# Wider buffers for split weights: 4128 bytes for 4096 in a two-layer decoder kernel

## The chip, the cores and the metric

The kernel runs on 1 core of a Trainium2 chip. The metric is the device time of one execution in microseconds, as the median of the runs. TensorE (PE) multiplies matrices, VectorE (DVE) and ScalarE (ACT) work elementwise, GpSimd (POOL) does a few small things, SyncE (SP) issues the DMAs that bring the weights. All operands of TensorE lie in the on-chip memory SBUF, which has 128 partitions; a place in it is a byte offset within each partition.

## What is computed

A decoder trunk of two layers on 512 tokens of 1024 features, all float32. Each layer is a half step of SwiGLU, a mixer (a pooling branch and an attention branch with 16 heads, merged by gates), and another half step of SwiGLU:

```python
def swiglu(x, w_gate, w_up, w_down):
    return (jax.nn.silu(x @ w_gate) * (x @ w_up)) @ w_down

for l in range(DEPTH):
    x = x + 0.5 * swiglu(rmsnorm(x, ffn1_norm[l]), ffn1_w_gate[l], ffn1_w_up[l], ffn1_w_down[l])
    proj = rmsnorm(x, mix_norm[l]) @ w_in[l]      # queries, keys, values, gates, pool input
    ...
    merged = g_pool * (o_pool @ w_branch_pool[l]) + g_attn * (o_nsa @ w_branch_nsa[l])
    x = x + merged @ w_out[l]
    x = x + 0.5 * swiglu(rmsnorm(x, ffn2_norm[l]), ffn2_w_gate[l], ffn2_w_up[l], ffn2_w_down[l])
return rmsnorm(x, final_norm)
```

The hidden width of SwiGLU is 2816.

## The kernel before

Activations are kept transposed, 128 features on the partitions and the 512 tokens along the free axis. A float32 product is made of three float32r passes over two-part splits of both operands: high times high, high times low, low times high. `mm3` (lines 110 to 117) issues them for each tile of 128 input features: line 114 multiplies the high weights `wh` with the high activations, line 115 `wh` with the low activations, line 116 the low weights `wl` with the high activations. The weights are the stationary operand (128 by 128, loaded into the array by a weight load ahead of each matmul) and the activations are the moving operand (512 columns that stream through). The weight load of the next matmul runs while the present one streams.

Weights come in blocks of 1 MB: `load` (line 88) issues one DMA on SP into one of three raw buffers `wr`; `wsplit` (line 95) cuts off a unit of 8 tiles of 128 by 128 (the last chunk of SwiGLU has units of 6 for the down projection), copies its high part on ACT (line 107) into one buffer of the tag `w` and takes the low part on DVE (line 108) into another. The tag `w` has six buffers, so three units are held at a time. `proj` (line 119) makes one output tile of 128 features from a unit, 24 matmuls for a unit of 8.

The order of the work is the order in which `run_steps` goes through a list of steps written out by hand; each unit's load and split are traced ahead of the matmuls of the unit before it. Three kinds of activations stand as the moving operand against units of the tag `w`: `xh`/`xl` (the gained and split input, tag `xg`, 16 buffers of 2048 bytes; also `oh`/`ol`, the attention output), `act` (SwiGLU's hidden tiles), `mh`/`ml` and `mixed` (these three in the large buffers of tag `A`). Gate and up projections, and the mixer's input projection `w_in`, move `xh`/`xl`; the down projection moves `act`.

The allocator puts the buffers one behind another, tag by tag in the order of first use, so what stands ahead of a tag fixes its place. All tags between `s` and `x` follow one another without gaps. From the built programs, places in bytes modulo 256 (a buffer's tiles of 512 or 2048 bytes have the same place as its start, modulo 256):

| tag | what | before | with the change |
|---|---|---|---|
| `A` | `act`, `mh`/`ml`, `mixed`, probabilities | 128 | 128 |
| `ident` | matrix for transposes | 128 | 128 |
| `wr` | raw weights | 32 | 32 |
| `w` buffers 0, 1, 2, 3, 4, 5 | split weights | 32 each | 32, 64, 96, 128, 160, 192 |
| `xg` | `xh`/`xl`, `oh`/`ol` | 32 | 224 |
| `x` | residual, queries `q` | 32 | 224 |
| `K`, `pr`, `V`, `pc`, `Kc` | keys, probabilities, values | 160 | 96 |

A unit's high and low part lie in buffers 0 and 5, 4 and 3, or 2 and 1, in turn.

Of the kernel before, what the change touches and what calls it, by code (L numbers as in the profile page):

```python
# [12 lines left out]
F32R = mybir.dt.float32r  # L13
# [38 lines left out]
class Trunk:  # L52
    """Activations are kept transposed: features on partitions, the 512 tokens
    along the free axis. A float32 product is three float32r passes over exact
    two-part splits of both operands (hi*hi + hi*lo + lo*hi)."""

# [10 lines left out]

# [1 line left out]
    def unit(self, tag, bufs, dt=F32, name=None, shape=(P, T)):  # L69
# [16 lines left out]

# [1 line left out]
    def load(self, src, kt, cols):  # L88
        """Rows (k p) of a [kt*128, cols] block onto partitions p."""
        raw = self.unit("wr", 3, F32, "wr", (P, 2048))  # L90
        v = raw[:, : kt * cols].rearrange("p (k c) -> p k c", k=kt)
        self.nc.sync.dma_start(v, src.rearrange("(k p) c -> p k c", p=P))
        return v

    def wsplit(self, v):
        """Exact split of a [128, a, b] weight block, a * b <= 1024."""
        a, b = v.shape[1], v.shape[2]
        out = []
        for nm in ("wh", "wl"):
            t = self.unit("w", 6, F32R, nm, (P, 1024))  # L100
            out.append(t[:, : a * b].rearrange("p (a b) -> p a b", a=a))
        hi, lo = out
        self.split(hi, lo, v)
        return hi, lo
# [5 lines left out]
    def mm3(self, out, terms, first=True, last=True):  # L110
        """out = sum over terms of lhsT^T rhs, each given as (lh, ll, rh, rl)."""
        n = len(terms)
        for i, (lh, ll, rh, rl) in enumerate(terms):
            self.nc.tensor.matmul(out, lh, rh, start=first and i == 0, stop=False)  # L114
            self.nc.tensor.matmul(out, lh, rl, start=False, stop=False)  # L115
            self.nc.tensor.matmul(out, ll, rh, start=False,  # L116
                                  stop=last and i == n - 1)

    def proj(self, tag, w, act):
        """One 128-feature output tile from a split weight unit."""  # L120
        out = self.bank(tag)
        hi, lo = w
        self.mm3(
            out,
            [(hi[:, k], lo[:, k], act[k][0], act[k][1]) for k in range(hi.shape[1])],
        )
        return out

# [1 line left out]
    def constants(self):  # L130
# [14 lines left out]
    def load_columns(self, names):  # L145
        """Per-feature vectors as columns, 128 features on partitions."""
        nc, io = self.nc, self.io
        rows = self.s("rows")[:, :P]
        r0 = min(ROWS[nm] for nm in names)
        n = 0  # L150
        for nm in names:
            src = io[nm]
            if nm == "cmp_pos":
                src = src.rearrange("l (a b) c -> (l a) (b c)", b=2)
            elif nm == "final_norm":
                src = src.rearrange("(k c) -> k c", c=P)
            else:
                src = src.rearrange("l (k c) -> (l k) c", c=P)
            r = ROWS[nm] - r0
            n = max(n, r + src.shape[0])  # L160
            nc.scalar.dma_start(rows[r : r + src.shape[0]], src)
        pt = self.bank("pv")
        nc.tensor.transpose(pt[:, :n], rows[:n], self.ident[:n, :n])
        nc.vector.tensor_copy(self.cols[:, r0 : r0 + n], pt[:, :n])

    def constants2(self):
        nc = self.nc

        def const(shape, name):
            return self.sb.tile(list(shape), F32, tag=name, name=name)  # L170

        # dist[p, c] = 384 + p - c, and MASKED where that is negative
        self.dist = const((P, T), "dist")
# [4 lines left out]
                                channel_multiplier=1)  # L178
        # distc[(j n), t] = t - (16 n + 31), and MASKED where that is negative
        self.distc = const((P, T), "distc")  # L180
        for j in range(4):
# [5 lines left out]
                                    channel_multiplier=-16)  # L187
        # qcol[(e d), m]: negated query scale over the slope of head 2 m + e
        self.qcol = const((P, ND), "qcol")
        for h in range(H):  # L190
            e = h % 2
            nc.gpsimd.memset(self.qcol[e * DH : e * DH + DH, h // 2 : h // 2 + 1],
                             -(DH ** -0.5) / SLOPES[h])
        # block[p, j] = 1 where p // 32 is j or j + 2
        self.block = const((P, 2), "block")
        nc.gpsimd.memset(self.block, 0.0)
        for j in range(4):
            nc.gpsimd.memset(self.block[32 * j : 32 * j + 32, j % 2 : j % 2 + 1], 1.0)
        # ramp[g, t] = w / (t + 1) for the first w tokens of pool group g
        self.ramp = const((P, 4, 16), "ramp")  # L200
# [4 lines left out]

# [1 line left out]
    def gain(self, x, col):  # L207
        """Split of x times its feature gain."""
        g = self.cols[:, col : col + 1]
# [8 lines left out]
    def norm_piece(self, d, x, row, split=True):  # L218
        """x[d] is final: gain it, split it, add its squares."""
        nc = self.nc  # L220
# [14 lines left out]
    def stats(self):  # L235
        """Per token 1/rms of the last normed activation, as columns per token
        block and (but after the last layer) along rows."""
        nc = self.nc
# [36 lines left out]

# [1 line left out]
    def run_steps(self, steps, nxt=0):  # L277
        """Steps are (fetch, run); each fetch is traced ahead of the run of the
        fetching step before it."""
        fetches = [i for i, (f, _) in enumerate(steps) if f]  # L280
        for i, (_, run) in enumerate(steps):
            while nxt < len(fetches) and (nxt == 0 or fetches[nxt - 1] <= i):
                steps[fetches[nxt]][0]()
                nxt += 1
            run()

    def units(self, src, n, kt, cols, cut, use, rows=False, pre=None):
        """Steps over n weight blocks [kt*128, cols], each cut into units of
        `cut` columns (or row tiles)."""
        steps = []  # L290
# [17 lines left out]

# [1 line left out]
    def ffn(self, wg, wu, wd, on_x):  # L310
# [41 lines left out]

# [1 line left out]
    def key_cmp_in(self, j, w):  # L354
        """Compressed-branch input as [(parity d), g, token pair]."""
        p = self.proj("mm", w, self.xg)
# [8 lines left out]
    def keys(self, br, w):  # L365
        """Keys stacked twice on partitions, hi and lo apart."""
        nc = self.nc
# [12 lines left out]
    def values(self, tb):  # L380
        """Values (stationary [keys, hi | lo]) and branch gates of a token block."""
        nc = self.nc
# [48 lines left out]
    def compress_steps(self, l, which):  # L431
        """MLP over the overlapping blocks of the compressed keys (which = 0) or
        values (1), the blocks stationary as [hi | lo]."""
        nc, io = self.nc, self.io
# [82 lines left out]

# [1 line left out]
    def pool_weights(self, l):  # L519
# [7 lines left out]
    def pool_unit(self, l, g, w):  # L527
        """Pool group g: trailing mean less the token, mixed and scaled."""
        nc = self.nc
# [28 lines left out]

# [1 line left out]
    def query_unit(self, m, w):  # L560
        """Per head of the pair the negated scaled query over the head's slope,
        [hi; lo] on partitions (odd heads [lo; hi])."""
        nc = self.nc
# [10 lines left out]
    def cmp_probs(self, qd):  # L574
        """Gated probabilities over the compressed keys of four heads, per head
        pair hi and lo stacked on partitions, [hi; lo] and [lo; hi]."""
        nc = self.nc
# [39 lines left out]
    def head_probs(self, h):  # L617
        """Gated probabilities of the selected and window branches, queries on
        partitions. The selection takes every block (8 of at most 16) and the
        window spans the sequence, so both attend to all keys up to the query."""  # L620
        nc = self.nc
# [72 lines left out]

# [1 line left out]
    def mixer(self, l, on_x):  # L696
# [110 lines left out]

# [1 line left out]
    def run(self):  # L809
# [103 lines left out]
```

## Time and profile before

| | |
|---|---|
| median of 2 runs | 2411.93 us (2410.0 to 2413.85) |
| span of the profiled execution | 2409.0 us |
| TensorE, matmuls | busy 2377.3 us (99%), 11042 matmuls |
| TensorE, weight loads | busy 1951.9 us (81%) |
| VectorE | 1398.9 us (58%) |
| ScalarE | 976.9 us (41%) |
| DMA | 31.6% of 16 engines, 101 GB/s from and to HBM |
| granted TensorE clock | 0.998 of full speed |

A matmul's busy time overlaps the next one's, since matmuls are pipelined: a single one is shown 389 ns long while the next starts 227 ns after it. The time that a matmul costs in a run of them is therefore read from start to start, called the step below, and not from its length. Lengths and steps go up and down together.

### The profile page before, as it was taken

The numbers are of one execution on the slowest core, as the hardware profiler recorded it, in microseconds if no ns is written. First come the engines' busy times: TensorE is split into PE (matmuls) and PEld (weight loads), VectorE is DVE, ScalarE is ACT, GpSimd is POOL, SyncE is SP. The second block draws the span as 40 slices with busy tenths as digits, with TensorE's granted clock in tenths as the row PEclk, the third lists the DMA queues.
The fourth block names the chain that finished last, engine by engine and source line by source line (L and its number), as shares of the span: only waits on it lengthen the run. The fifth ranks groups of instructions, "written<-read, shape, count | busy, mean of one in ns | idle before, by whom it ended". The sixth has DMA issues, their size and how long they took to land.

```text
span 2409.0 us, 28552 instructions
## 1 busy us (share of the span) xinstructions
PE 2377.3 (99%) x11042; PEld 1951.9 (81%) x11042; DVE 1398.9 (58%) x2684; ACT 976.9 (41%) x1689; POOL 51.5 (2%) x106
## 2 busy tenths in 40 slices
PE   8999999999999999999999999999999999999998
PEld 6888888788888888888888888887888887888887
DVE  4434347778988544443544443567988975434444
ACT  4222234566666422222432222445666753222222
POOL 1000000000001000000000000000000010000000
PEclk9999999999999999999999999999999999999999
DMA  5332324422125422323232323335222253232321
GB/s 158 98 95 95 97 89 147 141 98 71 49 79 167 135 88 91 102 90 98 92 104 89 96 97 96 119 108 160 69 68 79 75 184 105 89 103 88 105 79 62
DMA packets 226007, 244.24 MB, mean 101 GB/s; under 512 B 8688, under 2 KB 206416, under 8 KB 225872
## 3 DMA queue, kind: packets, MB, share of 16 engines
q1 hardware_dynamic: 225696, 242.37, 31.6%
q8 instruction: 87, 1.43, 0.3%
q14 instruction: 48, 0.39, 0.1%
q10 hardware_dynamic: 176, 0.05, 0.0%
HBM read 223.53 MB, written 18.87 MB: 101 GB/s over the span
## 4 chain that ended last, share of the span: by engine, by line
PE 58%; issue 15%; DVE 1%; POOL 1%; DMA 1%; ACT 0%; POOLq 0%; DVEq 0%; SPq 0%; ACTq 0%
PE ps_mm L116 9%; PE ps_mm L115 9%; PE ps_mm L114 9%; PE ps_pv L689 4%; PE ps_sc L114 3%; PE ps_sc L115 3%; PE ps_sc L116 3%; PE ps_pt L114 3%; PE ps_pt L115 3%; PE ps_pt L116 3%; PE ps_pt L675 3%; PE ps_sc L653 2%; PE ps_sc L643 1%; DMA bP<-dB 1%; PE ps_sc L582 0%
## 5 line engine op out<-in xcount | busy, mean ns | idle before, releaser
L107 ACT ACTIVATE wh<-wr 128x1024 fp32r<-128x1024 f32 (+1 forms) x392 | 408.8, 1043 | 1099.5 <-PE ps_mm L115 414.3
L108 DVE TENSOR_TENSOR wl<-wr,wh 128x1024 fp32r<-128x1024 f32 (+1 forms) x392 | 469.9, 1200 | 76.6 <-ACT wh L107 75.5
L116 PE MATMUL ps_mm<-act,wl 128*128 128x512 f32 x704 | 280.8, 399 | 0.0
L114 PE MATMUL ps_sc<-xh,wh 128*128 128x512 f32 x704 | 277.1, 394 | 2.2 <-ACT x L838 2.2
L115 PE MATMUL ps_mm<-act,wh 128*128 128x512 f32 x704 | 277.6, 394 | 0.0
L114 PE MATMUL ps_mm<-act,wh 128*128 128x512 f32 x704 | 275.5, 392 | 0.0
L115 PE MATMUL ps_sc<-xl,wh 128*128 128x512 f32 x704 | 274.5, 390 | 0.0
L116 PE MATMUL ps_sc<-xh,wl 128*128 128x512 f32 x704 | 274.2, 389 | 0.0
L114 PE MATMUL ps_pt<-xh,wh 128*128 128x512 f32 x704 | 273.9, 389 | 0.0
L115 PE MATMUL ps_pt<-xl,wh 128*128 128x512 f32 x704 | 273.9, 389 | 0.0
L116 PE MATMUL ps_pt<-xh,wl 128*128 128x512 f32 x704 | 273.9, 389 | 0.0
L340 DVE SCALAR_TENSOR_TENSOR x<-ps_mm,x 128x512 f32<-128x512 f32 x96 | 66.4, 691 | 253.8 <-PE ps_mm L116 253.8
L331 DVE TENSOR_TENSOR u<-ps_pt,R 128x512 f32<-128x512 f32 x88 | 60.9, 692 | 245.7 <-PE ps_pt L116 245.7
L114 PE MATMUL ps_mm<-xh,wh 128*128 128x512 f32 x512 | 203.4, 397 | 0.0
L323 DVE TENSOR_TENSOR z<-ps_sc,R 128x512 f32<-128x512 f32 x88 | 60.9, 692 | 243.1 <-PE ps_sc L116 243.0
L116 PE MATMUL ps_mm<-xh,wl 128*128 128x512 f32 x512 | 200.9, 392 | 0.0
L115 PE MATMUL ps_mm<-xl,wh 128*128 128x512 f32 x512 | 200.8, 392 | 0.0
L115 PEld LDWEIGHTS ps_mm<-act,wh 128*128 128x128 f32 x704 | 132.1, 188 | 34.7 <-DVE act L108 0.8
L114 PEld LDWEIGHTS ps_sc<-xh,wh 128*128 128x128 f32 x704 | 132.4, 188 | 31.5 <-ACT x L838 2.6
L114 PEld LDWEIGHTS ps_mm<-act,wh 128*128 128x128 f32 x704 | 132.2, 188 | 31.6
L116 PEld LDWEIGHTS ps_mm<-act,wl 128*128 128x128 f32 x704 | 132.2, 188 | 30.5
L634 ACT ACTIVATE tbuf<-tbuf,m 128x128 f32<-128x128 f32 (+3 forms) x256 | 142.1, 556 | 36.3 <-DVE m L632 28.4
(238 smaller groups left out, 3864.6 us busy)
## 6 DMA issues: line engine op xcount, KB each, us to landing
wr<-in_ffn_w_gate_dram SPq DMA_DIRECT2D x44, 1024.0 KB, 5.4
wr<-in_ffn_w_up_dram SPq DMA_DIRECT2D x44, 1024.0 KB, 5.4
wr<-in_w_in_dram SPq DMA_DIRECT2D x34, 1024.0 KB, 5.3
wr<-in_ffn_w_down_dram SPq DMA_DIRECT2D x32, 1024.0 KB, 4.9
wr<-in_ffn_w_down_dram SPq DMA_DIRECT2D x16, 768.0 KB, 4.2
wr<-in_w_branch_nsa_dram SPq DMA_DIRECT2D x8, 1024.0 KB, 5.2
wr<-in_w_out_dram SPq DMA_DIRECT2D x8, 1024.0 KB, 5.3
dx<-x SPq DMA_DIRECT2D x16, 256.0 KB, 2.7
```

The costliest lines, as they stand in the source:

```text
L107: self.nc.scalar.activation(hi, src, AF.Copy)
L108: self.nc.vector.tensor_sub(lo, src, f32(hi))
L114: self.nc.tensor.matmul(out, lh, rh, start=first and i == 0, stop=False)
L115: self.nc.tensor.matmul(out, lh, rl, start=False, stop=False)
L116: self.nc.tensor.matmul(out, ll, rh, start=False, stop=last and i == n - 1)
L323: nc.vector.tensor_mul(z, g, self.R)
L331: nc.vector.tensor_mul(u, up, self.R)
L340: nc.vector.scalar_tensor_tensor(x, o, 0.5, x, ALU.mult, ALU.add)
L634: nc.scalar.activation(t, t, AF.Exp, scale=-1.0, bias=m[:, i : i + 1], accum_out=c[:, i : i + 1])
L653: nc.tensor.matmul(sp, qq, K[:, br, :nk], start=i == 0, stop=i == 1)
L675: nc.tensor.transpose(tp[:, w : w + P], probs[qb, br][:, kb * P : kb * P + P], self.ident)
L689: nc.tensor.matmul(out[:, T - n :], lhsT, rhs, start=i == 0, stop=i == len(ops) - 1)
```

## The change

Each buffer of the tag `w` gets 1032 float32 elements on a partition for 1024. The units still use the first 1024 of them (or fewer), so each instruction reads and writes as much as before. The six buffers take 192 bytes more on each partition, and all that is allocated behind them moves up by 192 bytes. Comments and docstrings are left out, and a blank line is added ahead of the changed one, so that lines from 100 on have numbers that are higher by one.

```diff
     def wsplit(self, v):
-        """Exact split of a [128, a, b] weight block, a * b <= 1024."""
+
         a, b = v.shape[1], v.shape[2]
         out = []
         for nm in ("wh", "wl"):
-            t = self.unit("w", 6, F32R, nm, (P, 1024))
+
+            t = self.unit("w", 6, F32R, nm, (P, 1032))
             out.append(t[:, : a * b].rearrange("p (a b) -> p a b", a=a))
```

On every engine the same instructions stand in the same order with the same waits, and each tile is in the buffer with the same number as before.

## Rows read from the trace of the kernel before

**Rows 1.** The page: span, and busy time of each engine

```profile
span 2409.0 us, 28552 instructions
...
PE 2377.3 (99%) x11042; PEld 1951.9 (81%) x11042; DVE 1398.9 (58%) x2684; ACT 976.9 (41%) x1689; POOL 51.5 (2%) x106
```

**Rows 2.** Stretches: gate and up; down; mixer. Columns as in the heading row

```profile
core 0: us, PE busy (x) PEld busy (x) DVE busy (x) ACT busy (x) POOL busy (x), PEclk, DMA share, GB/s
30.00:108.00 78.00, 78.00 (x347) 64.55 (x346) 35.50 (x43) 22.92 (x28) 0.00 (x0) 1.00 0.30 96
109.00:153.00 44.00, 44.00 (x191) 35.37 (x190) 16.54 (x18) 9.12 (x9) 0.00 (x0) 1.00 0.30 91
...
385.00:750.00 365.00, 360.81 (x1896) 299.39 (x1895) 305.60 (x863) 224.72 (x514) 7.14 (x9) 1.00 0.30 94
```

**Rows 3.** Timeline of PE (start us, length us), up and gate: first and last of 178

```profile
299.67 0.39 PE L115 MATMUL ps_pt<-xl,wh 128*128 128x512 f32 x1
...
339.79 0.39 PE L115 MATMUL ps_sc<-xl,wh 128*128 128x512 f32 x1
```

**Rows 4.** Timeline of PE, down projection: first four and last of 169

```profile
244.73 0.39 PE L115 MATMUL ps_mm<-act,wh 128*128 128x512 f32 x1
244.97 0.40 PE L116 MATMUL ps_mm<-act,wl 128*128 128x512 f32 x1
245.20 0.39 PE L114 MATMUL ps_mm<-act,wh 128*128 128x512 f32 x1
245.43 0.39 PE L115 MATMUL ps_mm<-act,wh 128*128 128x512 f32 x1
...
283.93 0.39 PE L115 MATMUL ps_mm<-act,wh 128*128 128x512 f32 x1
```

**Rows 5.** Instructions on tile wl: length ns min/median/max, first and last start us

```profile
L116 PE MATMUL ps_sc<-xh,wl x704: 387/389/628, 17.0 to 2351.1; 128*128 128x512 f32 x176
L116 PEld LDWEIGHTS ps_pt<-xh,wl x704: 187/188/188, 33.2 to 2361.7; 128*128 128x128 f32 x176
...
L116 PEld LDWEIGHTS ps_mm<-act,wl x704: 187/188/190, 109.3 to 2395.3; 128*128 128x128 f32 x176
L116 PE MATMUL ps_mm<-act,wl x704: 393/399/399, 109.6 to 2395.6; 128*128 128x512 f32 x176
...
L116 PE MATMUL ps_mm<-xh,wl x512: 387/389/500, 385.2 to 1934.8; 128*128 128x512 f32 x171
...
L116 PE MATMUL ps_mm<-oh,wl x128: 388/389/402, 748.7 to 1983.9; 128*128 128x512 f32 x128
...
L116 PE MATMUL ps_mm<-mh,wl x128: 394/399/399, 796.8 to 2030.1; 128*128 128x512 f32 x128
...
L116 PE MATMUL ps_mm<-mixed,wl x64: 388/394/497, 468.6 to 1683.0; 128*128 128x512 f32 x64
```

**Rows 6.** Timeline of PE, an input projection in the mixer, after attention's matmuls

```profile
660.14 0.39 PE L115 MATMUL ps_mm<-xl,wh 128*128 128x512 f32 x1
660.37 0.40 PE L116 MATMUL ps_mm<-xh,wl 128*128 128x512 f32 x1
...
661.75 0.39 PE L116 MATMUL ps_mm<-xh,wl 128*128 128x512 f32 x1
...
664.47 0.39 PE L116 MATMUL ps_mm<-xh,wl 128*128 128x512 f32 x1
```

**Rows 7.** Timeline of PE where the down projection hands over to gate

```profile
285.80 0.40 PE L114 MATMUL ps_sc<-xh,wh 128*128 128x512 f32 x1
...
287.65 0.39 PE L116 MATMUL ps_sc<-xh,wl 128*128 128x512 f32 x1
287.88 0.39 PE L114 MATMUL ps_sc<-xh,wh 128*128 128x512 f32 x1
288.11 0.39 PE L115 MATMUL ps_sc<-xl,wh 128*128 128x512 f32 x1
288.33 0.39 PE L116 MATMUL ps_sc<-xh,wl 128*128 128x512 f32 x1
```

**Rows 8.** The page's groups (count, busy us, mean ns, idle before): matmuls

```profile
L114 PE MATMUL ps_mm<-act,wh 128*128 128x512 f32 x704 | 275.5, 392 | 0.0
L115 PE MATMUL ps_sc<-xl,wh 128*128 128x512 f32 x704 | 274.5, 390 | 0.0
...
L114 PE MATMUL ps_mm<-xh,wh 128*128 128x512 f32 x512 | 203.4, 397 | 0.0
...
L115 PE MATMUL ps_mm<-xl,wh 128*128 128x512 f32 x512 | 200.8, 392 | 0.0
```

**Rows 9.** Groups with shapes kept apart: two of attention's matmuls

```profile
L653 PE MATMUL ps_sc<-KL,q 128*128 128x512 f32 x64 | 25.1, 392 | 0.0
...
L582 PE MATMUL ps_sc<-q,Kc 128*128 128x512 f32 x64 | 16.6, 396 | 0.0
```

**Rows 10.** The page's groups: the weight split

```profile
L107 ACT ACTIVATE wh<-wr 128x1024 fp32r<-128x1024 f32 (+1 forms) x392 | 408.8, 1043 | 1099.5 <-PE ps_mm L115 414.3
L108 DVE TENSOR_TENSOR wl<-wr,wh 128x1024 fp32r<-128x1024 f32 (+1 forms) x392 | 469.9, 1200 | 76.6 <-ACT wh L107 75.5
```

## The prediction

> **What bounds the kernel now.** I read the engines' busy times first: TensorE is busy in 2377.3 of 2409.0 us, VectorE in 1398.9, ScalarE in 976.9 [rows 1]. Then stretches, to see whether that holds everywhere: in SwiGLU's projections TensorE is busy throughout (78.00 of 78.00 and 44.00 of 44.00 us) while VectorE and ScalarE work less than half the time, and in the mixer it is busy in 360.81 of 365.00 us with VectorE at 305.60 [rows 2]. The granted clock is full (1.00), that is 2.4 GHz, in all three [rows 2]. So nothing feeds TensorE too slowly; what a matmul takes from its start to the next one's start, the step, makes the time.
>
> The third view is the timeline, for the step. In up and gate 178 matmuls of 512 columns start between 299.67 and 339.79 us: 40.12 us over 177 steps, 226.7 ns each [rows 3]. In the down projection 169 matmuls of the same shape start between 244.73 and 283.93 us: 39.20 us over 168 steps, 233.3 ns [rows 4]. Neither waits for anything, both load a 128 by 128 tile beside each matmul in 187 to 190 ns [rows 5], and still one is 6.6 ns slower. The lengths say the same: 389 ns at the median in gate, 399 on line 116 of down [rows 5].
>
> The fourth view asks what differs. It isn't the PSUM tile: the mixer's input projection writes ps_mm as down does, and once it has settled it takes 2.72 us for the 12 steps from 661.75 to 664.47, again 226.7 ns [rows 6]. It isn't the weights either, which come the same way into the same six buffers. By tile the 512-column matmuls fall into two classes: those that move xh/xl or oh/ol have a median of 389 ns, those that move act, mh or mixed one of 394 to 399 [rows 5]. By the table of places the first lie at 32 modulo 256, where all six weight buffers lie too, and the second at 128. So the slower class is the one whose moving operand and weights lie at different places, here 96 bytes apart.
>
> The fast step is something that the stream falls into, not something that each matmul has. After attention's matmuls, the input projection needs 1.61 us for its first 7 steps (230.0 ns) before it goes at 226.7 [rows 6]; where gate follows down, 1.85 us go into the first 8 steps (231.3 ns), and the next three take 0.68 us (226.7) [rows 7]. With equal places, then, "in step" is 226.7 and "out of step" about 231; with places 96 bytes apart the stream doesn't reach the fast step in 169 matmuls [rows 4].
>
> **What the change does.** It adds no instruction, moves none, and takes no wait away. It puts the weights at six places and, through the 192 bytes ahead of them, xh/xl at 224. No weight buffer then lies at the place of xh/xl: they are 32 to 192 bytes behind it. For act, mh and mixed, which stay at 128, one buffer of six (number 3) lies at the same place. High and low weights of a unit always lie at different places, so the distance changes from matmul to matmul.
>
> *Matmuls that lose the common place.* Gate and up: six groups of 704 two of them in [rows 5, 8], 4224 matmuls. What a step costs out of place isn't in the trace for these distances. The nearest rows: 233.3 ns at 96 bytes, settled [rows 4]; 231.3 ns at equal places but out of step [rows 7]; attention's keys and queries lie 128 bytes apart and have mean lengths of 392 and 396 [rows 9], which is 3 and 7 over the 389 of gate. I take the middle of the first two, 232.3, so 5.6 ns more: 4224 x 5.6 = 23.7 us. Bounds: nothing (226.7 at any place), and 10 ns (every matmul as long as line 116 in down, 399 for 389).
>
> The input projections in the mixer, three groups of 512 [rows 5, 8], have means of 397 and 392 against a median of 389: about half are out of step already since attention's matmuls stand between them. I let the other half, 768, lose 5.6 ns: 4.3 us. The attention output oh/ol, three groups of 128, one of them in [rows 5], is at 389 mostly: 384 x 5.6 = 2.1 us.
>
> *Matmuls that were out of place before.* Down has three groups of 704 [rows 5, 8], mh/ml three of 128 and mixed three of 64, one of each in [rows 5]: 2688. Their step goes from 233.3 to 232.3 for five loads of six; for the sixth, at the common place, I take half of the 6.6 ns, since the stream needs some 8 matmuls to fall into step and the place changes within three. Mean gain (5 x 1.0 + 3.3) / 6 = 1.4 ns, 3.7 us. Bounds: 6.6 ns gained by all (17.7 us), and 4 ns lost (their mean of 395 going to 399), 10.8 us.
>
> *At nothing.* The split writes wh and wl at new places, 1043 and 1200 ns a unit [rows 10]. ScalarE is idle for 1099.5 us ahead of it, mostly waiting for TensorE to free a buffer [rows 10], and VectorE has 59.4 us free even in the mixer's 365 [rows 2]; were a split 5% longer there, TensorE's matmuls would still hide it. Attention's keys, probabilities and values all move by the same 192 bytes, and q too, so their distances stay; only the transposes against ident (fixed at 128) keep what they had, since their other operand lies in tag A. The loops of values, compression and pool mix (some 340 matmuls of 256 to 512 columns in both layers) get other distances; at 5 ns each that is under 2 us to either side, and I leave it out. The DMAs write where they did, or 192 bytes on.
>
> *Sum.* 23.7 + 4.3 + 2.1 - 3.7 = 26.4 us. On the profiled execution's 2409.0 us that is 2435.4; the median of the runs is 2.9 us above that span, so 2438 us, 1.1% slower. A few us of the mixer's 4.3 may vanish in its waits.
>
> **Rivals.**
>
> *Place makes no difference.* The 6.6 ns of down could come from something else that act, mh and mixed share, being tiles of the large buffers; or the stream could fall into step whatever the distance. For the second: a unit of 24 would pay 8 out-of-step matmuls at 4.6 ns, 37 ns over 368 units (8832 / 24), 13.6 us, against the 17.7 us that tag A gains: -4 us. Either way about 2408 to 2412 us. Against the second stands that down never falls into step. The Trainium skill speaks for the first: "TensorE: Matmul & The Clock Gate", Part 2, step 1, says that TensorE reads the moving operand and the weights through two independent ports, so that loading the next weights takes nothing from the running matmul, and "SBUF — State Buffer", Who interferes with whom, that TensorE never waits for anyone. By that rule the sum is zero and the time 2411.9. The trace doesn't bear it out: one shape, one clock, no waits, and steps of 226.7 and 233.3 ns [rows 3, 4]. Chance 0.18.
>
> *Spreading ends a collision, faster.* If it is the common place that costs, and both 226.7 and 233.3 contain collisions that other distances avoid, every step could shrink. The shortest lengths seen are 387 for 389 [rows 5], so 224.7 ns: 4224 x 2 = 8.4 us, some 5.8 us in the mixer's 1920 (about 3 ns each, half of them being out of step), and 2688 x 8.6 = 23.1 us in tag A, in all 37 us: 2375 us. It decides from the point where most of the distances of 32 to 192 bytes give less than 226.7. Against it: the one settled distance in the trace that isn't zero is slower, and so are the unsettled ones at 128 bytes [rows 9]. For 2% each of the 8832 matmuls would have to gain 5.5 ns (48.2 us / 8832), which no row shows. The page on TensorE (the Trainium skill, Back-to-back matmuls in Part 1) gives 215.7 ns for 512 columns; were that reached, it would be an estimate of 115 us less, 2297. Chance 0.10, 0.04 of it beyond 2%.
>
> *The wrong distances are worse than 96 bytes.* At 399 ns throughout, 53.8 us (5376 x 10) + 10.8 us: 2476 us, 2.7% slower. For it: line 116 of down is at 399 in nearly every case [rows 5], so such collisions exist at one distance, and with a distance that changes each matmul the stream may never settle. Against it: the two matmuls beside it, lines 114 and 115, are at 392 and 394 [rows 8]. Chance 0.14 for more than 2460.
>
> **How the numbers follow.** Forecast (2420 to 2460) 0.58, no difference 0.18, faster 0.10, over 2460 0.14. The likeliest is 2438. The range goes from 2400, below which only the better part of the faster case lies (0.09), to 2465 (about 0.10 above). 2% is 48 us, 2364 and 2460, and about what a measurement of this kernel can tell from no change: faster 0.04, same 0.82, slower 0.14.
>
> **What the next profile would show.** Right: gate's and up's matmuls, 389 at the median, at 392 to 397, with a pattern that repeats every three units as the buffers do; steps of about 232 ns; down slightly shorter than 392/394/399; weight loads at 188 still; TensorE's idle time, the order and the clock as before. Wrong: gate's matmuls still at 389 (place doesn't matter, or the stream falls into step anywhere), lengths under 387 (spreading helps), or 400 and more. If lengths stay and the time moves, the cause lies elsewhere: in the split on VectorE or in new waits of TensorE.

## The result and the profile after

The changed kernel takes 2442.26 us (2442.07 to 2442.44), the kernel before 2411.93, that is 30.3 us or about 1.3% more. The ratio on record is 1.0129 with a 95% interval of 1.0099 to 1.0158; the ratios on record, here and below, can differ by up to a thousandth from the quotient of the two medians. The forecast was 2438.

The page of the changed kernel, span and busy times:

```profile
span 2440.7 us, 28552 instructions
...
PE 2409.8 (99%) x11042; PEld 1957.0 (80%) x11042; DVE 1400.0 (57%) x2684; ACT 977.1 (40%) x1689; POOL 51.9 (2%) x106
```

Against [rows 1] the span grew by 31.7 us and TensorE's busy time by 32.5; VectorE and ScalarE do the same work in the same time (1.1 and 0.2 us more). The engine that bounds the kernel got slower; the other engines' busy times hardly moved.

The timeline of TensorE in up and gate (start us, length us), first four and last of 173 matmuls of the changed kernel:

```profile
299.70 0.39 PE L116 MATMUL ps_sc<-xl,wh 128*128 128x512 f32 x1
299.93 0.39 PE L117 MATMUL ps_sc<-xh,wl 128*128 128x512 f32 x1
300.16 0.39 PE L115 MATMUL ps_pt<-xh,wh 128*128 128x512 f32 x1
300.39 0.40 PE L116 MATMUL ps_pt<-xl,wh 128*128 128x512 f32 x1
...
339.78 0.40 PE L117 MATMUL ps_sc<-xh,wl 128*128 128x512 f32 x1
```

40.08 us over 172 steps are 233.0 ns, where [rows 3] gave 226.7. In the down projection (first and last of 187):

```profile
244.69 0.40 PE L116 MATMUL ps_mm<-act,wh 128*128 128x512 f32 x1
...
287.83 0.40 PE L116 MATMUL ps_mm<-act,wh 128*128 128x512 f32 x1
```

43.14 us over 186 steps, 231.9 ns, for 233.3 in [rows 4]. The lengths say it too, in the view of the instructions on tile wl (ns min/median/max):

```profile
L117 PE MATMUL ps_sc<-xh,wl x704: 388/397/628, 18.2 to 2382.6; 128*128 128x512 f32 x176
L117 PEld LDWEIGHTS ps_pt<-xh,wl x704: 187/188/188, 32.4 to 2393.6; 128*128 128x128 f32 x176
...
L117 PE MATMUL ps_mm<-act,wl x704: 389/396/402, 110.9 to 2427.2; 128*128 128x512 f32 x176
```

Gate's median went from 389 to 397 and down's line from 399 to 396 [rows 5]; a weight load still takes 188 ns. What is drawn out is the matmul that runs beside it. Such lengths are a hint and not a measure of the step: they don't always go up and down with it, as the experiments show.

Where the 31.7 us are, by stages of the timeline (from the last matmul of one down projection to the first gate matmul of the next SwiGLU, and so on):

| stretch | before | changed | difference |
|---|---|---|---|
| start and first SwiGLU, layer 1 | 384.5 | 389.3 | 4.8 |
| mixer, layer 1 | 456.6 | 465.5 | 8.9 |
| second SwiGLU of layer 1, first of layer 2 | 730.7 | 742.2 | 11.5 |
| mixer, layer 2 | 458.5 | 459.3 | 0.8 |
| second SwiGLU, layer 2, and the end | 378.6 | 384.4 | 5.8 |

The SwiGLU stretches grew by 22.1 us together, where the sum had 20.7 (23.7 for gate and up, less 3.0 for down). The two mixers do the same work, yet one grew by 8.9 us and the other by 0.8; that needs a reason of its own. Stretches of the changed kernel in layer 1's mixer (columns: us, busy us of each engine with counts, granted clock, DMA share, GB/s) and the view of tile w2r, a 64 KB load for the compression (first the SP issues, then what its first reader waited for, and the time from issue to landing):

```profile
490.00:495.00 5.00, 2.74 (x11) 2.07 (x11) 1.06 (x4) 1.29 (x5) 0.00 (x0) 0.86 0.15 52
495.00:500.00 5.00, 5.00 (x17) 4.28 (x17) 1.57 (x5) 2.53 (x5) 0.00 (x0) 0.50 0.00 0
500.00:505.00 5.00, 5.00 (x15) 3.91 (x14) 0.92 (x2) 0.09 (x1) 0.00 (x0) 0.62 0.27 105
505.00:510.00 5.00, 5.00 (x24) 4.08 (x23) 1.13 (x1) 2.14 (x3) 0.00 (x0) 1.00 0.13 52
```

```profile
L479 SPq DMA_DIRECT2D w2r<-in_cmp_v_w_dram x2: 384/384/384, 485.2 to 1692.9; - x2
its engine sat idle before it (us, times) until:
  DMA w2r<-in_cmp_v_w_dram: 2.7, 2
...
DMA to landing us min/median/max: 3.3/4.9/7.9
```

```profile
493.14 0.31 ACT L108 ACTIVATE w2h<-w2r 128x128 fp32r<-128x128 f32 x1 [2.37 <-DMA w2r<-in_cmp_v_w_dram]
...
493.55 0.36 PE L115 MATMUL ps_pv<-w2h,hh 128*128 128x64 f32 x1 [2.26 <-issue]
```

The last fence is the timeline around 493 us. The load landed late: ScalarE stood idle for 2.37 us until it came, and TensorE for 2.26 us. (For TensorE the profile names no cause, but its matmul reads the copy w2h, which ScalarE ended at 493.45 us.) Behind that idle time the granted clock was at 0.50 from 495 to 500 us, the lower of its two levels (1.2 GHz), and at 0.62 on average from 500 to 505: 17 and 15 matmuls in 5 us where the next 5 us hold 24. Whether this belongs to the change, the experiments with an early load say.

### The profile page after: what moved, and what is told of

Read it like the earlier page. It is cut to its first block, busy times and chain, and to the rows that moved or that the text cites. A ratio compares the mean times of both kernels' runs of the same rounds, so it can differ in the third digit from the quotient of the medians.

```text
span 2440.7 us, 28552 instructions
## 1 busy us (share of the span) xinstructions
PE 2409.8 (99%) x11042; PEld 1957.0 (80%) x11042; DVE 1400.0 (57%) x2684; ACT 977.1 (40%) x1689; POOL 51.9 (2%) x106
## 4 chain that ended last, share of the span: by engine, by line
PE 58%; issue 15%; DVE 1%; ACT 0%; POOL 0%; POOLq 0%; DVEq 0%; ACTq 0%
PE ps_mm L117 9%; PE ps_mm L116 9%; PE ps_mm L115 9%; PE ps_pv L690 3%; PE ps_sc L117 3%; PE ps_sc L115 3%; PE ps_sc L116 3%; PE ps_pt L117 3%; PE ps_pt L115 3%; PE ps_pt L116 3%; PE ps_pt L676 3%; PE ps_sc L654 2%; PE ps_sc L644 1%; PE ps_sc L583 0%; POOL ec L606 0%
## 5 line engine op out<-in xcount | busy, mean ns | idle before, releaser
L108 ACT ACTIVATE wh<-wr 128x1024 fp32r<-128x1024 f32 (+1 forms) x392 | 408.7, 1043 | 1126.5 <-PE ps_mm L116 414.1
L117 PE MATMUL ps_sc<-xh,wl 128*128 128x512 f32 x704 | 279.4, 397 | 0.0
L115 PE MATMUL ps_pt<-xh,wh 128*128 128x512 f32 x704 | 278.8, 396 | 0.0
L116 PEld LDWEIGHTS ps_sc<-xl,wh 128*128 128x128 f32 x704 | 133.1, 189 | 32.3 <-issue 1.0
L117 PEld LDWEIGHTS ps_sc<-xh,wl 128*128 128x128 f32 x704 | 132.7, 188 | 32.5
L116 PEld LDWEIGHTS ps_mm<-act,wh 128*128 128x128 f32 x704 | 132.0, 188 | 32.7 <-DVE act L109 0.9
L117 PEld LDWEIGHTS ps_pt<-xh,wl 128*128 128x128 f32 x704 | 132.1, 188 | 32.4
```

The costliest lines, as they stand in the source:

```text
L108: self.nc.scalar.activation(hi, src, AF.Copy)
L117: self.nc.tensor.matmul(out, ll, rh, start=False, stop=last and i == n - 1)
```

## The experiments

The theory from the prediction: what sets the step is the distance, modulo 256 bytes, between the place of the moving operand and that of the weights; zero is the fast one. Pads are tiles that nothing writes or reads; they move what is allocated behind them. Each kernel differs from the kernel before by the lines shown, unless it says otherwise.

**All operands at one place.** If the distance is what counts, tag A's matmuls should become fast as well when weights and xh/xl are moved to its 128. In `wsplit`, ahead of the first buffer of the tag `w`:

```diff
+        if "pad1" not in self.__dict__:
+            self.pad1 = self.sb.tile([P, 24], F32, tag="pad1", name="pad1")
```

> A pad of 96 bytes ahead of the tag w: all six weight buffers and xh/xl/oh/ol lie at 128 modulo 256, where act, mh/ml and mixed lie already; all buffers 4096 bytes as before. Theory (the distance between moving operand and weights, modulo 256, sets the step; zero is the fast one): gate and up stay at 226.7 ns a step, down, mh/ml and mixed fall from 233.3 to 226.7, lengths 389 everywhere; 2688 x 6.6 ns = 17.7 us less, 2394 us. Rival (the place itself, 128 for 32, is bad): gate and up go to 233.3 as down has it, 2440 us. Rival (only places that differ within a unit cost): no change, 2412 us.

2397.01 us, ratio 0.9936 (0.9921 to 0.9952) to the kernel before. The instructions on wl:

```profile
L118 PE MATMUL ps_pt<-xh,wl x704: 389/389/389, 32.1 to 2349.5; 128*128 128x512 f32 x176
...
L118 PE MATMUL ps_mm<-act,wl x704: 387/389/402, 108.3 to 2382.4; 128*128 128x512 f32 x176
```

Down (first and last of 161 in its timeline):

```profile
244.72 0.39 PE L117 MATMUL ps_mm<-act,wh 128*128 128x512 f32 x1
...
280.99 0.39 PE L118 MATMUL ps_mm<-act,wl 128*128 128x512 f32 x1
```

36.27 us over 160 steps, 226.7 ns. Down is at 389 like gate and up, whose place changed by 96 bytes without a change in length. The place itself doesn't matter, the distance does. The time is 3 us above the forecast of 2394; the experiments with an early load tell why.

**Distance without spreading.** All six weight buffers at 32, 4096 bytes each, and xh/xl where the change puts them; in `gain`, ahead of the first buffer of the tag `xg`:

```diff
+        if "pad2" not in self.__dict__:
+            self.pad2 = self.sb.tile([P, 48], F32, tag="pad2", name="pad2")
         hi = self.unit("xg", 16, F32R, "xh")
```

> Six weight buffers of 4096 bytes, all at 32 as before, but a pad of 192 bytes behind them, so that xh/xl and all tags behind lie where the change puts them (224). Theory (distance alone): gate and up leave the fast step although all weights lie at one place, to about 232 to 236 ns, 2440 us (2432 to 2455); down stays at 392/394/399. Rival (it is the spreading of the six, high and low at different places, that costs): gate and up stay at 226.7, 2412 us.

2445.37 us, ratio 1.0135 (1.012 to 1.015). Gate's and up's matmuls leave 389 (first up's and down's lines on wl, then first and last of 173 in the timeline of gate and up):

```profile
L116 PE MATMUL ps_pt<-xh,wl x704: 393/394/398, 32.4 to 2398.5; 128*128 128x512 f32 x176
L116 PE MATMUL ps_mm<-act,wl x704: 388/392/403, 110.8 to 2432.1; 128*128 128x512 f32 x176
```

```profile
299.81 0.39 PE L116 MATMUL ps_sc<-xh,wl 128*128 128x512 f32 x1
...
339.94 0.39 PE L114 MATMUL ps_sc<-xh,wh 128*128 128x512 f32 x1
```

40.13 us over 172 steps are 233.3 ns for gate and up. Moving xh/xl alone costs as much as the whole change, though the weights lie at one place. Down stays: its median on this line is 392 for 399, but its three lines have only swapped (394, 399 and 392 for 392, 394 and 399), and its step is 233.3 still, 32.20 us over 138 from 249.65 to 281.85. Spreading isn't needed for the loss.

**Spreading without the move.** The changed kernel with the same lines and 16 elements for 48, so that xh/xl lie at 32 again.

> The changed kernel with a pad of 64 bytes behind the weights, so that xh/xl and all behind lie at 32, 96 and 160 modulo 256 as before; the six weight buffers lie at 32 to 192. Theory (distance): five of six buffers still lie elsewhere than xh/xl, gate and up stay at about 231 to 233 ns, 2435 us (2428 to 2445). Rival (xh/xl at 224, or what moved behind it, is what costs): gate and up go back to 226.7, 2409 us.

2434.62 us (2433.91 to 2435.76), ratio 1.0091 (1.0074 to 1.0108). Spreading alone loses too, although one buffer in six, the first, then has the place of xh/xl; the time is that of the changed kernel once late loads are out of the way (2434.95, below). So both halves of the change are enough by themselves.

**Is it 256?** The kernel before with 64 elements as pad behind the weights: same place modulo 256, another modulo 512.

> Six weight buffers of 4096 bytes at 32, and a pad of 256 bytes behind them: xh/xl lie at 32 modulo 256, but 256 bytes further modulo 512 and more. If the pattern repeats every 256 bytes: lengths of 389 in gate and up and 2412 us, as before. If it repeats only after 512 bytes or more: gate and up leave 226.7, 2430 to 2450 us.

2411.66 us (2409.28 to 2420.71), ratio 1.0003 (0.9991 to 1.0015). Up, on line 116:

```profile
L116 PE MATMUL ps_pt<-xh,wl x704: 389/389/389, 32.4 to 2371.9; 128*128 128x512 f32 x176
```

A shift by 256 bytes makes no difference to the step. The profiled run is the slowest, 2420.71 us; in it the copies of w2r waited 4.3 us for late loads like the one above.

**Every distance.** Four kernels with pads of n bytes both ahead of and behind the weights give gate and down each a new distance, all weights at one place (n is 32, 64, 128 and 160).

```diff
+            self.pad1 = self.sb.tile([P, n // 4], F32, tag="pad1", name="pad1")
 ...
+            self.pad2 = self.sb.tile([P, n // 4], F32, tag="pad2", name="pad2")
```

> Pads of 32 bytes ahead of and behind the weights (six buffers of 4096 bytes, all at one place): gate and up move operands 32 bytes further than the weights modulo 256, down 64. Theory (only a distance of zero gives the fast step): gate and up at 229 to 236 ns a step, lengths of 392 to 399, down about 233; 2425 to 2455 us. Rival (what the fast step wants is less than a whole 256, or near places do as well): gate and up at 226.7, 2412 us.

> Pads of 64 bytes ahead of and behind the weights: gate and up at a distance of 64 bytes, down at 32. Theory: gate and up at 229 to 236 ns, down at 229 to 236; 2425 to 2455 us. Rival (the pattern repeats every 64 bytes): gate and up at 226.7.

> Pads of 128 bytes ahead of and behind the weights: gate and up at a distance of 128 bytes, down at 224 (that is 32 to the other side). Theory: gate and up at 229 to 236 ns; 2425 to 2455 us. Rival (the pattern repeats every 128 bytes): gate and up at 226.7, 2412 us.

> Pads of 160 bytes ahead of and behind the weights: gate and up at a distance of 160 bytes, down at 192. Theory: gate and up at 229 to 236 ns, down, at the distance that gate and up have in the run with xh/xl 192 bytes behind, at its 233.3; 2425 to 2455 us. Rival: some distance beats zero, under 226 ns.

One run each, so without an interval: 2435.25, 2425.94, 2438.63 and 2447.99 us, the kernel before 2410.22 beside them. The timeline of TensorE of the one with 64 bytes, up and gate (first and last of 177), then down (first and last of 138), then its line on wl in up; last, up and gate of the one with 160 bytes (first and last of 173):

```profile
299.69 0.39 PE L117 MATMUL ps_pt<-xl,wh 128*128 128x512 f32 x1
...
339.98 0.39 PE L116 MATMUL ps_sc<-xh,wh 128*128 128x512 f32 x1
```

```profile
249.80 0.39 PE L118 MATMUL ps_mm<-act,wl 128*128 128x512 f32 x1
...
281.77 0.40 PE L117 MATMUL ps_mm<-act,wh 128*128 128x512 f32 x1
```

```profile
L118 PE MATMUL ps_pt<-xh,wl x704: 388/394/395, 31.8 to 2377.1; 128*128 128x512 f32 x176
```

```profile
299.67 0.39 PE L116 MATMUL ps_sc<-xh,wh 128*128 128x512 f32 x1
...
339.96 0.40 PE L117 MATMUL ps_sc<-xl,wh 128*128 128x512 f32 x1
```

40.29 us over 176 steps, 228.9 ns at a distance of 64; 31.97 over 137, 233.4 at 32; 40.29 over 172, 234.2 at 160. The line on wl has a median of 394 at 228.9 ns, and the same line with xh/xl 192 behind has 394 at 233.3: lengths and steps do not always go up and down together, as was said ahead of the change, and the table goes by steps. Read in the same way from all kernels (distance: moving operand minus weights, modulo 256):

| distance | gate and up, ns | down, ns |
|---|---|---|
| 0 | 226.7 (before) | 226.7 (all at one place) |
| 32 | 233.4 (32) | 233.4 (64) |
| 64 | 228.9 (64) | 228.9 (32) |
| 96 | | 233.3 (before) |
| 128 | 233.4 (128) | |
| 160 | 234.2 (160) | |
| 192 | 233.3 (192 behind) | 233.3 (160) |
| 224 | | 233.3 (128) |

In brackets stands the kernel, by its pad. Each figure is from one stretch of 30 to 45 us; the means over the whole traces lie within 0.3 ns of it, but for 128 (232.9). Gate and down agree at the four distances where both were measured, though they move different tiles into different PSUM tiles. No distance beats zero, and none but 64 comes near. The expectation of 229 to 236 held for all but 64, which is a shade below it.

The table comes near the change's size on average, but not unit by unit. In the changed kernel a unit multiplies its high part twice and its low part once, and the two lie at different distances. The timeline of the changed kernel holds three units of 24 matmuls in up and gate, and three in down; each row is the first matmul of a unit (the last row that of the next):

```profile
305.76 0.40 PE L115 MATMUL ps_pt<-xh,wh 128*128 128x512 f32 x1
311.35 0.40 PE L115 MATMUL ps_sc<-xh,wh 128*128 128x512 f32 x1
316.94 0.39 PE L115 MATMUL ps_sc<-xh,wh 128*128 128x512 f32 x1
322.54 0.40 PE L115 MATMUL ps_pt<-xh,wh 128*128 128x512 f32 x1
```

```profile
250.03 0.39 PE L115 MATMUL ps_mm<-act,wh 128*128 128x512 f32 x1
255.61 0.39 PE L115 MATMUL ps_mm<-act,wh 128*128 128x512 f32 x1
261.15 0.39 PE L115 MATMUL ps_mm<-act,wh 128*128 128x512 f32 x1
266.71 0.40 PE L115 MATMUL ps_mm<-act,wh 128*128 128x512 f32 x1
```

| buffers of the unit (high, low) | gate: distances | by the table | seen | down: distances | by the table | seen |
|---|---|---|---|---|---|---|
| 0, 5 | 192, 192, 32 | 233.3 | 232.9 | 96, 96, 192 | 233.3 | 230.8 |
| 4, 3 | 64, 64, 96 | 230.4 | 232.9 | 224, 224, 0 | 231.1 | 231.7 |
| 2, 1 | 128, 128, 160 | 233.7 | 233.3 | 32, 32, 64 | 231.9 | 232.5 |

The means by the table are 232.5 for gate (233.0 was measured) and 232.1 for down (231.9). But gate's unit at 64 is not the fast one, and down is fastest where none of its distances is zero or 64; over all units of the trace the means are 233.1, 232.9 and 233.1 for gate and 231.4, 231.7 and 232.5 for down. Pairing each moving operand with the weights that are loaded beside it, those of the next matmul, doesn't help, since a unit's three distances stay the same. So the table holds where every matmul has the same distance. Where the distance changes within three matmuls, a step depends on more than its own distance, and how is not shown.

**The late load.** The load of w2r is issued where it is needed, behind transfers of 1 MB. Here it is issued some steps ahead, into a buffer of its own; first in the kernel with all operands at 128, beside that kernel without it, then in the kernel before and the changed one.

```diff
             if i == 0:
                 st["hid"] = self.bank("sc")
+            if i == 2 * which:
+                st["w2r"] = self.unit("w2r", 1, F32, "w2r", (P, 128)).rearrange(
+                    "p (c d) -> p c d", c=2)
+                nc.sync.dma_start(st["w2r"], w2.rearrange("(c p) d -> p c d", p=P))
 ...
-        w2r = self.s("w2r")[:, :128].rearrange("p (c d) -> p c d", c=2)
-        nc.sync.dma_start(w2r, w2.rearrange("(c p) d -> p c d", p=P))
```

> The kernel with all operands at 128 modulo 256, and the small load of the compression's second weights (w2r) issued some steps ahead, into a buffer of its own, instead of where it is needed, behind transfers of 1 MB. In some profiles, those of the kernel before not among them, TensorE stands idle 1.3 to 2.9 us for that load once or twice and its granted clock then falls to half for up to 10 us. Theory: these idle stretches are no part of the change to places, cost some 2 us each and 5 us more where the clock falls, and go away: 2385 to 2392 us, and a narrower spread than the 2392.92 to 2401.75 of the kernel without it. Rival (the idle stretches cost nothing in most runs): 2397 us as without it.

> The kernel with all operands at 128 modulo 256 once more, on the same chip as the one with the early load: 2397 us (2392 to 2402), 0.6% under the kernel before.

2391.18 us (2390.55 to 2392.38), ratio 0.9914 (0.9901 to 0.9928), with the early load; 2396.0 (2390.53 to 2401.24), 0.9933 (0.9918 to 0.9948), without. The group of the matmul that waited, without and with (count, busy us, mean ns, idle us before):

```profile
L116 PE MATMUL ps_pv<-w2h,hh 128*128 128x64 f32 x8 | 2.3, 281 | 4.3 <-issue 4.3
```

```profile
L116 PE MATMUL ps_pv<-w2h,hh 128*128 128x64 f32 x8 | 2.0, 244 | 0.0
```

The idle time is gone and the spread of the runs shrinks from 10.7 to 1.8 us, with the same fastest run: the late load strikes some runs and not others. With the early load the kernel lies 2.8 us under the 2394 forecast for it, without it 2 to 3 us over.

> The kernel before (all weights and xh/xl at 32, act at 128) with the compression's second weights loaded ahead. The profile of before shows TensorE idle for that load for 0.3 us in all. Theory: little to gain where the load mostly arrives in time, 2408 us (2404 to 2411). Rival (most of its unprofiled runs hold such idle stretches too): 2403 us or less.

> The changed kernel (six places) with the same early load. Its profile has one idle stretch of 2.3 us there, and a granted clock at half for 10.2 us behind it. Theory (places alone cost 24.8 us in gate and up and about 3 net elsewhere, the idle stretch and the clock are a matter of when transfers land): 2435 us (2431 to 2438), and 26 to 29 us above the kernel before with the early load. Rival (the change itself brings that stretch, and slower steps cost the whole 30 us): 2442 us still, or a difference of over 30.

2409.0 us, ratio 0.9997 (0.9988 to 1.0006), for the kernel before with the early load: nothing to gain in the median, though its runs now lie between 2408.45 and 2410.13 where without the early load they go from 2408.04 to 2415.02. 2434.95 us, 1.0108 (1.0091 to 1.0125), for the changed one: some 7 us below its 2442.26. The two were not measured beside each other and the intervals of their ratios overlap, so that the load makes this difference rests on the traces: by the same stretches as above the change costs 5.8, 2.0, 11.5, 0.8 and 5.8 us, and layer 1's mixer has lost its extra. Free of late loads the change costs 25.95 us, just under the 26 to 29 expected.

## Why the prediction was right, point by point

**What bounds, and what differs.** Right, and now shown: the class of matmuls with another place than the weights is the slow one because of the distance and not because of its tiles. Moved to one place with the weights, it goes at gate's step, 226.7 ns.

**Matmuls that lose the common place.** The step came out at 233.0 for the 232.3 chosen between 231.3 and 233.3, that is 6.3 ns more for 5.6. The middle of two rows of another kind had no ground of its own, and that it came so near is in part luck: at one distance for all, gate's step goes from 228.9 to 234.2. All of SwiGLU together (gate, up and down) grew by 5.8 + 11.5 + 5.8 = 23.1 us in the pair with the early load; the sum had 23.7 less down's 2112 x 1.4 = 3.0, so 20.7. The term was a little small.

**Down.** The number is right to the tenth, 1.4 ns gained, 233.3 to 231.9, but its reasons were not borne out, and the fit is luck. Five of six loads were to gain 1.0 ns each and the one at the common place 3.3. That one is a low part, one matmul in nine and not one load in six. And the gain is not where it was put: the unit with buffers 0 and 5, whose distances (96 and 192) gain nothing in the table, gains most, 2.1 ns in the mean over the trace (233.5 to 231.4).

**The mixer.** The sum put 4.3 + 2.1 us there, less tag A's share of 576 x 1.4 = 0.8: 5.6 us in both layers. With the early load the two mixers grew by 2.0 and 0.8. The matmuls did get slower (in the input projections the page after has mean lengths of 400 and 395 on lines 115 and 116, for 397 and 392 in [rows 8]), but only half of the forecast arrived; that the rest vanished in the mixer's waits, as the sum's last line allowed, fits and was not taken apart.

**The sum.** 26.4 us were forecast, 25.95 are measured once the late load is out of the way. The other few us of the 30.3 are not in the sum at all: a wait for a 64 KB load, 0.4 us in the trace of before and 2.7 in that of the changed kernel, and the lower clock behind it. TensorE's idle time and the clock, which the next profile was to show as before, were not as before. The prediction looked for waits that the change adds in the code, and there are none; it didn't look for those that the kernel has already and that sit near their limit. So the fit of 26.4 to 25.95 is in part luck too: SwiGLU was 2.4 us too low and the mixers 2.8 us too high. And the fit of 2438 to 2442 hides a wait that was not in the sum.

**At nothing.** Right for the split, which takes 1043 and 1200 ns as before:

```profile
L109 DVE TENSOR_TENSOR wl<-wr,wh 128x1024 fp32r<-128x1024 f32 (+1 forms) x392 | 470.0, 1200 | 78.6 <-ACT wh L108 77.2 <-PE ps_mm L117 0.4
L108 ACT ACTIVATE wh<-wr 128x1024 fp32r<-128x1024 f32 (+1 forms) x392 | 408.7, 1043 | 1126.5 <-PE ps_mm L116 414.1 <-PE ps_pt L116 320.2 <-issue 215.6
```

**The rivals.** That place makes no difference fell with the changed kernel itself and with the table: the same load beside the same matmul gives steps up to 7.5 ns apart (226.7 and 234.2), by distance alone. The page's rule (the Trainium skill, "TensorE: Matmul & The Clock Gate", Part 2, step 1), that loading the next weights takes no SBUF read bandwidth from the running matmul, had spoken for this rival; whether it is read bandwidth that is short here, no run shows. That the stream falls into step at any distance fell with the table. Faster by spreading: no distance of the eight is under 226.7. Worse than 96 bytes: 234.2 at 160 is the worst, 0.9 ns over it, and even that kernel took 2447.99 us, not 2460. The 399 of line 116 was no sign of worse places: with xh/xl 192 behind, line 115 has it and down's step is the same.

**What stays open.** Why zero is the fast distance and 64 nearly so isn't shown; distances other than multiples of 32 bytes weren't tried. How a step comes about where the distance changes from matmul to matmul is open as well. Nor is it settled why the late load struck the changed kernel, by its times in both runs, and the kernel before in some at most.

## What to carry to other kernels

Where TensorE streams back to back and its step is over what the same shape takes elsewhere in the trace, compare the places of moving operand and weights modulo 256 bytes: the same place for both cost a pad of 96 bytes here and brought 0.6%. Padding every buffer by a little, so that they lie at different places, did the opposite of that (1.1% slower without late loads), and the allocator passes such a pad on to all that lies behind it. And before a forecast in a kernel that is full to 99%, look for small loads issued where they are needed: the kernel with one place for all and that load issued early is the fastest of all, 2391.18 us, 0.9% under the kernel before.

## What the runs showed of the hardware

The step of a 512-column float32r matmul with a 128 by 128 weight load beside it depends on where its two operands lie: 226.7 ns at a distance of 0 modulo 256 bytes, 228.9 at 64, 233.3 to 234.2 at 32, 96, 128, 160, 192 and 224, all buffers at one distance. At the four distances where two kinds of tiles were measured they agree. The weight load itself takes 187 or 188 ns at the median in each. Where three matmuls in a row have two distances, the steps of these distances do not carry over (232.9 ns for a unit at 64, 64 and 96). TensorE's idle stretch of 2.26 us in the changed kernel was followed by about 10 us at the lower clock (0.50 granted from 495 to 500 us, 1.00 again from 505).
